# Two hybrid diffusion layers on one core: probabilities scaled by ScalarE and VectorE, output groups in turn, and a reordered start

## The chip, the core and the metric

The kernel runs on one core of a Trainium2 chip. Its time is the device time of one execution in microseconds; each figure for "time" is a median over runs. The trace comes from one separate, profiled execution.

## The reference: what is computed

Two layers over 384 tokens (128 context, 256 latent) of width 1024, in fp32. A layer is: a SwiGLU FFN (hidden width 2816) at half weight, a token mixer, and a second FFN; each takes an RMS-normalised input that is scaled and shifted by adaLN vectors, and each output is gated by one of them.

```python
mod = jax.nn.silu(cvec) @ lp["ada_w"] + lp["ada_b"]
sh1, sc1, g1, sh2, sc2, g2, sh3, sc3, g3 = jnp.split(mod[:, None, :], N_ADA, axis=-1)
h = _rmsnorm(x, lp["norm_g"][0]) * (1.0 + sc1) + sh1
x = x + 0.5 * g1 * _swiglu(h, w1[0], w3[0], w2[0])
h = _rmsnorm(x, lp["norm_g"][1]) * (1.0 + sc2) + sh2
y, ctx = mixer(h)
x = x + g2 * y
```

The mixer projects `h` once and feeds three groups: Hyena (256 channels: a short convolution, then a long one by FFT with a generated filter, two gates), neighbourhood attention N (6 heads of 64, a learned bias over the latent grid), and windowed attention G (6 query heads, 2 key heads, rotary, a sink). Latent tokens also read all cached context keys in the same softmax. The three outputs, 1024 wide together, go through one output projection.

## The kernel before, in words

Tokens are the free dimension: the state is `xT[0..7]`, eight chunks of 128 channels by 384 tokens. Every fp32 product is three TensorE passes in fp32r (`mm3`, lines 291 to 295): high half by high half, and the two mixed ones. Weights arrive by SP's DMA queue into one of three raw buffers in the order of the list `jobs` (lines 135 to 150); `ahead` (line 162) splits them three blocks ahead into `whi` (ScalarE, line 132) and `wlo` (VectorE, line 133). The split stands in the queues of these two engines at the place where `ahead` is called, so the written order is the order of each engine.

adaLN's vectors are 256 reductions on VectorE (`junk`, line 196). `ada_tick` calls them at the rates `RATE` and `MIXRATE`; `need` calls those that are due and not done. The first FFN's own vectors come from TensorE in three chunks (`adm`) whose weights `chunk_load` fetches.

The order of a layer is `ffn(l, 0)`, `mixer(l)`, `ffn(l, 1)`. An FFN begins with eight dense steps `k` of six outputs each, whose inputs are the halves `mh[k]`, `ml[k]`; statistics are taken after step 2 (`stats1`, a sum by TensorE, then an rsqrt by Newton steps that POOL does) and spread over the partitions after step 4 (`stats2`: `dg`, then `pr`). In the very first FFN, `start` is called ahead of each step: it holds the filter generator of Hyena (`first` to `fourth`, `taps`, eight calls of `spectrum`, line 593) and the normalisation of the input (`start_x`, `start_h`).

The mixer first does Hyena's projection: two groups `grp` of four weight blocks `kb`, into six accumulators. Then generators of small steps run beside the matmuls (`work`, `drain`): the convolution and FFT of Hyena, and the normalisation of queries and keys. The projections are called in the order q, k, (kv, gq); gq are the queries of G, which `rot` turns into `ra`, TensorE transposes into `gt`, and ScalarE copies into `qTG`.

Attention is a pipeline over 12 units: N then G, three head pairs, two blocks of 128 queries. The unit with `qi` = 0 also holds the context's queries, so it has n = 2 score blocks, the one with `qi` = 1 has n = 1. Call number s of `slot` does, in this order: scores and masks of unit s (`un_score`), the division by the sum of unit s-1 (`un_norm`, on POOL, line 899), the product with the values of unit s-3 if that had `qi` = 1 (`un_pv`, which ends with `yh`, `yl`), the transposes of unit s-2 and their copies `PT` (`un_turn`, lines 960 to 965), the exponentials of unit s (`un_exp`).

The output projection has three groups of output chunks: 0 to 2, 3 to 5, and 6, 7. `piece(po, g, k)` adds input chunk k to group g between slots: 2 to 7 come from attention, 0 and 1 from Hyena. The pieces of groups 0 and 1 alternate, k = 0 and 1 come last. `update` (line 370) adds a finished chunk to `xT` and `after` calls `square_chunk` and `prep_chunk`, which make the second FFN's `mh`, `ml`.

## Time and profile before

| | |
|---|---|
| median of 3 runs | 1580.31 us (1577.92 to 1580.56) |
| the profiled execution | 1582.27 us, of which the span is 1580.5 |
| mean granted TensorE clock | 0.985 |
| TensorE busy | 1518.8 us (96%), 8616 matmuls |
| VectorE, ScalarE, POOL busy | 1109.9, 675.9, 148.8 us |
| HBM traffic | 257.34 MB read, 164 GB/s over the span |

A row of a timeline begins with start and length in us, then engine, line of the program, operation, tiles and shape; a bracket at its end is the idle time before it and what ended that. "PEld" is the loading of weights into TensorE, "SPq" SP's queue of DMA issues. A pass of the large products is short against its listed length, since passes overlap: what counts is the distance between starts.

### The profile page before, as it was taken

The numbers are of one execution on the slowest core, as the hardware profiler recorded it, in microseconds if no ns is written. First come the engines' busy times: TensorE is split into PE (matmuls) and PEld (weight loads), VectorE is DVE, ScalarE is ACT, GpSimd is POOL, SyncE is SP. The second block draws the span as 40 slices with busy tenths as digits, with TensorE's granted clock in tenths as the row PEclk, the third lists the DMA queues.
The fourth block names the chain that finished last, engine by engine and source line by source line (L and its number), as shares of the span: only waits on it lengthen the run. The fifth ranks groups of instructions, "written<-read, shape, count | busy, mean of one in ns | idle before, by whom it ended". The sixth has DMA issues, their size and how long they took to land.

```text
span 1580.5 us, 23068 instructions
## 1 busy us (share of the span) xinstructions
PE 1518.8 (96%) x8616; PEld 1446.2 (92%) x8616; DVE 1109.9 (70%) x2048; ACT 675.9 (43%) x1237; POOL 148.8 (9%) x266
## 2 busy tenths in 40 slices
PE   6999999999989899999999999999998889999999
PEld 2899999999767799999999999999996689999998
DVE  4469998878765588877858898887776367644433
ACT  4633333336554554333335333343564555433321
POOL 0000000011543000000000000000145500000000
PEclk9999999999999899999999999999998999999999
DMA  9555666565412245655544565556452033433442
GB/s 305 187 189 214 233 229 217 215 212 155 139 36 75 97 138 195 231 210 186 200 145 140 204 245 199 214 203 217 144 162 66 25 113 127 148 137 129 126 140 68
DMA packets 89720, 261.46 MB, mean 165 GB/s; under 512 B 10182, under 2 KB 27656, under 8 KB 89480
## 3 DMA queue, kind: packets, MB, share of 16 engines
q1 hardware_dynamic: 89224, 258.95, 47.8%
q8 instruction: 67, 1.10, 0.3%
q0 software_dynamic: 384, 1.05, 0.2%
q14 instruction: 45, 0.37, 0.1%
HBM read 257.34 MB, written 2.62 MB: 164 GB/s over the span
## 4 chain that ended last, share of the span: by engine, by line
PE 82%; DVE 7%; ACT 6%; POOL 2%; issue 2%; DMA 1%; SPq 0%; DVEq 0%; ACTq 0%; POOLq 0%
PE up L293 14%; PE up L294 14%; PE up L295 14%; PE dn L294 8%; PE dn L293 8%; PE dn L295 8%; PE pj L293 2%; PE pj L295 2%; PE pj L294 2%; DVE wlo L133 2%; POOL pr L899 1%; ACT whi L132 1%; PE sc L911 1%; PE kf L593 1%; PE hy L293 1%
## 5 line engine op out<-in xcount | busy, mean ns | idle before, releaser
L133 DVE TENSOR_TENSOR wlo<-raw,whi 128x1024 fp32r<-128x1024 f32 (+2 forms) x352 | 395.3, 1126 | 170.2 <-ACT whi L132 169.7
L293 PE MATMUL up<-mh,whi 128*128 128x384 f32 (+1 forms) x1408 | 481.0, 342 | 13.4 <-DVE xT L373 6.4
L132 ACT ACTIVATE whi<-raw 128x1024 fp32r<-128x1024 f32 (+2 forms) x352 | 340.9, 976 | 323.6 <-DMA raw<-w 120.8
L295 PE MATMUL up<-mh,wlo 128*128 128x384 f32 (+1 forms) x1408 | 478.2, 340 | 1.0 <-DVE wlo L133 0.8
L294 PE MATMUL up<-ml,whi 128*128 128x384 f32 (+1 forms) x1408 | 477.6, 339 | 0.6 <-DVE ml L133 0.6
L196 DVE CUSTOM_DVE_ANT_0 junk<-adaw,cb,sml 128x1024 bf16<-128x1024 f32 x256 | 332.5, 1299 | 2.2
L293 PEld LDWEIGHTS up<-mh,whi 128*128 128x128 f32 x1408 | 266.2, 189 | 20.2 <-issue 9.3
L295 PEld LDWEIGHTS up<-mh,wlo 128*128 128x128 f32 x1408 | 266.2, 189 | 3.9 <-DVE wlo L133 3.9
L294 PEld LDWEIGHTS up<-ml,whi 128*128 128x128 f32 x1408 | 266.1, 189 | 2.2 <-DVE ml L133 1.3
L294 PE MATMUL dn<-gl,whi 128*128 128x384 f32 x704 | 237.2, 337 | 0.0
L293 PE MATMUL dn<-gh,whi 128*128 128x384 f32 x704 | 237.1, 337 | 0.0
L295 PE MATMUL dn<-gh,wlo 128*128 128x384 f32 x704 | 237.1, 337 | 0.0
L132 ACT ACTIVATE gh<-t 128x384 fp32r<-128x384 f32 x76 | 39.9, 525 | 247.2 <-DVE t L473 239.0
L293 PEld LDWEIGHTS dn<-gh,whi 128*128 128x128 f32 x704 | 132.2, 188 | 0.0
L295 PEld LDWEIGHTS dn<-gh,wlo 128*128 128x128 f32 x704 | 132.2, 188 | 0.0
L294 PEld LDWEIGHTS dn<-gl,whi 128*128 128x128 f32 x704 | 132.1, 188 | 0.0
L303 POOL TENSOR_SCALAR rs_r<-rs_r 128x3 int32<-128x3 int32 (+2 forms) x14 | 6.4, 460 | 1080.3 <-DVE rs_r L302 989.2
L899 POOL TENSOR_SCALAR pr<-pr,nm 128x384 f32<-128x384 f32 x72 | 78.8, 1112 | 65.5 <-DVE nm L896 29.5
L293 PE MATMUL pj<-whi,mh 128*128 128x384 f32 (+1 forms) x240 | 81.1, 338 | 2.0 <-DVE hyt L350 1.1
L295 PE MATMUL pj<-whi,ml 128*128 128x384 f32 (+1 forms) x240 | 78.9, 329 | 0.0
L294 PE MATMUL pj<-wlo,mh 128*128 128x384 f32 (+1 forms) x240 | 78.7, 328 | 0.0
L473 DVE TENSOR_TENSOR t<-up,t 128x384 f32<-128x384 f32 x72 | 39.9, 554 | 49.8 <-PE up L295 49.7
(220 smaller groups left out, 1618.0 us busy)
## 6 DMA issues: line engine op xcount, KB each, us to landing
raw<-w SPq DMA_DIRECT2D x184, 512.0 KB, 4.4
adaw<-ada SPq DMA_DIRECT2D x128, 512.0 KB, 3.5
raw<-w SPq DMA_DIRECT2D x64, 448.0 KB, 4.3
raw<-win SPq DMA_DIRECT2D x48, 384.0 KB, 3.6
raw<-w13a SPq DMA_DIRECT2D x32, 384.0 KB, 4.0
adw<-ada SPq DMA_DIRECT2D x32, 192.0 KB, 4.6
raw<-woa SPq DMA_DIRECT2D x16, 384.0 KB, 3.3
nab<-nab SPq DMA_DIRECT2D x24, 192.0 KB, 3.5
```

The lines of the kernel that those rows point to most:

```text
L132: S.activation(hi, src, AF.Copy)
L133: V.tensor_tensor(lo, src, hi.bitcast(F32), op=ALU.subtract)
L196: V.tensor_tensor_reduce(out=junk, in0=w, in1=cb[:, v, :], scale=scale, scalar=small("ada_b", (l * NADA + p) * KD + j), op0=ALU.mult, op1= ...
L293: T.matmul(out, ah, bh, start=start, stop=False)
L294: T.matmul(out, ah, bl, start=False, stop=False)
L295: T.matmul(out, al, bh, start=False, stop=stop)
L303: G.tensor_scalar(r.bitcast(I32), r.bitcast(I32), -1.0, float(0x5F3759DF), op0=ALU.mult, op1=ALU.add)
L473: V.tensor_tensor(t1, PQ[1][:, :NT], t1, op=ALU.mult)
L593: T.matmul(o, mat[:, 0:1] if row else mat, self.sd[t][:, which].rearrange("p l c -> p (l c)"), start=(n == 0), stop=(n == len(mats) - 1),)
L899: nc.gpsimd.tensor_scalar(pr[:, :w], pr[:, :w], rec[:, e * n + c:e * n + c + 1], None, op0=ALU.mult)
L911: T.matmul(u.sc[e][:, :NT], q[o[e], qs], k1[o[e]], start=True, stop=True)
```

## The change

1. **Rates** of the adaLN reductions: a little more in the first FFN of layer 0, less in the mixer.
2. **Hyena's projection**: statistics after the second block, their rsqrt on VectorE, `stats2` after the third, then `explicit`, `settle` and `deferred` spread over the rest.
3. **Weight order** follows the order of the projections and of the output pieces.
4. **Start**: all squares ahead of the third sine layer, statistics and the first table chunk earlier, `taps(2)` later, the eight spectra each in the middle of one of the eight dense steps.
5. **Convolution**: the first tap on ScalarE.
6. **Scaling of the probabilities**: on ScalarE for units with n = 1 (two operations each), on VectorE for units with n = 2 (four each).
7. **Projections** in the order q, k, gq, kv.
8. **Output groups**: only group 0 has pieces between the slots (k = 2 to 7); Hyena's k = 0, 1 follow, updates 0 to 2; then the whole of group 1 and updates 3 to 5; then group 2 and updates 6, 7.

```diff
--- before.py
+++ after.py
@@ -28,13 +28,12 @@
...
 NADAB = 3
-RATE = ((0.8, 0.72), (0.63, 0.515), (0.69, 0.66), (0.065, 0))
-MIXRATE = ((0.75, 0, 0.5), (0.3, 0, 0.3))
+RATE = ((0.82, 0.74), (0.63, 0.515), (0.69, 0.66), (0.065, 0))
+MIXRATE = ((0.25, 0, 0.5), (0, 0, 0.3))
 BUD = (2.0, 3.0, 1.9)
...
 DLATE = 8
-HYS = (1, 0)
 STAT = ((0, 2), (2, 4))
...
@@ -140,12 +139,12 @@
...
             if f == 0:
-                for g in (0, 1, 2, 3, 6, 5, 4):
+                for g in (0, 1, 2, 3, 5, 6, 4):
                     if g == 6:
...
                         jobs += [(A["win"][l, g, :, k * 768:(k + 1) * 768], 768) for k in range(4)]
-                for g, k in ((0, 1), (0, 2), (0, 3), (1, 1), (1, 2), (1, 3), (0, 0), (1, 0)):
+                for g, k in ((0, 1), (0, 2), (0, 3), (0, 0), (1, 0), (1, 1), (1, 2), (1, 3)):
                     jobs.append((A["woa"][l, g, :, k * 768:(k + 1) * 768], 768))
...
@@ -523,6 +522,8 @@
...
             self.decay = [decay[:, t * HY:(t + 1) * HY] for t in range(3)]
+
+        def load_d(self):
             self.dft0 = load(A["dft0"][:, 0:2 * P], tt("dft0", w=2 * P))
...
@@ -570,7 +571,7 @@
...
             if t < 2:
-                p0 = [ps("tap0") for _ in range(DEPTH)]
+                p0 = [ps("tap0", "a") for _ in range(DEPTH)]
                 for l in range(DEPTH):
...
@@ -660,7 +661,9 @@
...
             w3 = [small("conv_w", (l * 3 + q) * 6 + n) for q in range(3)]
-            V.tensor_scalar(o[:, 1:386], up[:, 0:385], w3[0], small("conv_b", l * 6 + n), op0=ALU.mult, op1=ALU.add)
+            S.activation(
+                o[:, 1:386], up[:, 0:385], AF.Identity, scale=w3[0], bias=small("conv_b", l * 6 + n)
+            )
             for q in (1, 2):
...
@@ -677,20 +680,18 @@
...
                 ahead()
-                if (grp, kb) == (0, HYS[0]):
-                    rs = stats1()
-                if (grp, kb) == (0, 3):
-                    dg = spread_r(rs)
-                ada_tick(MIXRATE[l][grp])
-                if (grp, kb) == (1, HYS[1]):
-                    R = stats2(rs, dg)
-                if grp == 1 and kb > HYS[1]:
-                    n = KD // (3 - HYS[1]) if HYS[1] != 0 else 3
-                    c = kb - HYS[1] - 1
-                    hn = explicit(l, 1, R, range(n * c, min(n * c + n, KD)))
-                    settle(hk)
-                    hk = hn
-                    tm[c] = deferred(pu[c], R, "hyt")
+                s = grp * 4 + kb
+                if s == 1:
+                    dg = spread_r(stats1(V))
+                elif s == 2:
+                    R = stats2(None, dg)
+                if s < 3:
+                    ada_tick(MIXRATE[l][0])
+                elif s < 6:
+                    hk += explicit(l, 1, R, range(3 * (s - 3), min(3 * (s - 2), KD)))
+                if s > 4:
+                    settle(hk[3 * (s - 5):3 * (s - 4)])
+                    tm[s - 5] = deferred(pu[s - 5], R, "hyt")
...
@@ -699,8 +700,6 @@
...
         def conv_bg():
-            settle(hk)
-            yield 1.0
             for n in [n for n in range(6) if n not in tm]:
...
@@ -896,7 +895,11 @@
...
                 for c, (pr, w) in enumerate(u.pr[e]):
-                    nc.gpsimd.tensor_scalar(pr[:, :w], pr[:, :w], rec[:, e * n + c:e * n + c + 1], None, op0=ALU.mult)
+                    r = rec[:, e * n + c:e * n + c + 1]
+                    if n == 1:
+                        S.activation(pr[:, :w], pr[:, :w], AF.Copy, scale=r)
+                    else:
+                        V.tensor_scalar(pr[:, :w], pr[:, :w], r, None, op0=ALU.mult)
...
@@ -1084,24 +1087,33 @@
...
+        pg = project(384, 2, BUD[0])
+        gq_it = add(gq_post(pg), True)
         pkv = project(256, 4, BUD[1])
         gk_it = add(gk_post(pkv), True)
-        pg = project(384, 2, BUD[0])
-        gq_it = add(gq_post(pg), True)
-
-        held = {}
-
-        def piece(po, g, k):
-            kb, kk = divmod(k, 2)
-            if (g, kb) not in held:
-                held[g, kb] = get()
-            hi, lo = held[g, kb]
+
+        def wout_block(po, n, kper, ks, first, last, run=True):
+            hi, lo = get()
+            for kk, i in order2(kper, n, last):
+                s = slice((kk * n + i) * P, (kk * n + i + 1) * P)
+                mm3(
+                    po[i][:, :NT], (hi[:, s], lo[:, s]), Y[ks + kk], first and kk == 0, last and kk == kper - 1
+                )
+            if run:
+                ahead()
+
+        held = []
+
+        def piece(po, k):
+            if not held:
+                held.append(get())
+            hi, lo = held[0]
             for i in range(3):
-                s = slice(kk * 384 + i * P, kk * 384 + (i + 1) * P)
-                mm3(po[i][:, :NT], (hi[:, s], lo[:, s]), Y[k], k == 2, k == 1)
-            if kk:
-                del held[g, kb]
-            ahead(state["cur"] + min(AHEAD, NSPL - len(held)))
+                s = slice(((k % 2) * 3 + i) * P, ((k % 2) * 3 + i + 1) * P)
+                mm3(po[i][:, :NT], (hi[:, s], lo[:, s]), Y[k], k == 2, False)
+            if k % 2:
+                held.pop()
+            ahead()
...
@@ -1111,49 +1123,35 @@
...
         nc.gpsimd.dma_start(out=A["o_nv"][l], in_=X["vN"][0])
-        po = [[ps(f"po{i}", "a") for i in range(3)]]
+        po = [ps(f"po{i}", "a") for i in range(3)]
         slot()
-        piece(po[0], 0, 2)
+        piece(po, 2)
         slot()
+        drain(gq_it)
         drain(gk_it)
-        drain(gq_it)
-        for k in (3, 4, 5):
+        for k in (3, 4, 5, 6):
             slot()
-            piece(po[0], 0, k)
+            piece(po, k)
             slot()
         slot()
-        piece(po[0], 0, 6)
-        slot()
-        spare[0] = "a"
-        po.append([ps(f"po{i}", "b") for i in range(3)])
-        piece(po[1], 1, 2)
-        slot()
-        for g, k in ((1, 3), (0, 7), (1, 4), (1, 5), (1, 6), (1, 7)):
-            piece(po[g], g, k)
-            work(BUD[2])
-            ada_tick(MIXRATE[l][2])
+        piece(po, 7)
         drain(hy_it)
-        for g in range(2):
-            for k in range(2):
-                piece(po[g], g, k)
-            for i in range(3):
-                update(l, 5, 3 * g + i, po[g][i])
-                after(3 * g + i)
-        po = [ps(f"po{i}", "ab"[i]) for i in range(2)]
-        for kb in range(2):
-            hi, lo = get()
-            for kk, i in order2(4, 2, kb == 1):
-                k = kb * 4 + kk
-                s = slice((kk * 2 + i) * P, (kk * 2 + i + 1) * P)
-                mm3(po[i][:, :NT], (hi[:, s], lo[:, s]), Y[k], k == 0, k == KD - 1)
-            if kb == 0:
-                ahead()
-                ada_tick(MIXRATE[l][2])
-        for i in range(2):
-            update(l, 5, 6 + i, po[i])
-            after(6 + i)
+        wout_block(po, 3, 2, 0, False, True, False)
+        for i in range(3):
+            update(l, 5, i, po[i])
+            after(i)
             if i == 0:
                 ahead()
+        for g, n, kper in ((1, 3, 2), (2, 2, 4)):
+            po = [ps(f"po{i}", "b" if g == 1 else "ab"[i]) for i in range(n)]
+            for kb in range(KD // kper):
+                wout_block(po, n, kper, kb * kper, kb == 0, kb == KD // kper - 1, kb < KD // kper - 1)
+                ada_tick(MIXRATE[l][2])
+            for i in range(n):
+                update(l, 5, 3 * g + i, po[i])
+                after(3 * g + i)
+                if i == 0:
+                    ahead()
...
@@ -1174,6 +1172,7 @@
...
                 chunk_rows((j + 2) // 3)
+            F.spectrum(*divmod(j, 3))
             return
...
@@ -1184,35 +1183,30 @@
...
             chunk_load(0)
+            F.load_d()
             issue(2)
...
             F.second()
-            square_chunk(4)
+            for c in range(4, KD):
+                square_chunk(c)
             F.third()
-            for c in range(5, KD):
-                square_chunk(c)
+            r = stats1()
             F.fourth()
...
             F.taps(0)
-            r = stats1()
             F.taps(1)
-            F.taps(2)
-            chunk_load(1)
             ada_tables(0)
-            F.spectrum(0, 0)
-            F.spectrum(0, 1)
-            F.spectrum(0, 2)
+            chunk_rows(0)
             R = stats2(r)
-            ahead(1)
-            chunk_rows(0)
             for c in range(3):
                 start_x(c, R)
-            F.spectrum(1, 0)
+            chunk_load(1)
             chunk_cols(0)
-            F.spectrum(1, 1)
+            ahead(1)
             start_h(0)
+            F.taps(2)
             start_h(1)
...
@@ -1224,8 +1218,6 @@
...
             start_h(j + 1)
-        if j < 4:
-            F.spectrum(*((1, 2), (2, 0), (2, 1))[j - 1])
         if j == 6:
...
         elif j == 7:
```

Three places of the engines' orders. First, ScalarE in the attention of layer 0, among the G units; `yh<-py` is the input of an output piece, `PT` the copy of the transposes, `pr` a unit's probabilities. Before:

```order
L945 ACTIVATE pr_4605,nm<-pr_4605,nm 128x384
L945 ACTIVATE pr_4606,nm<-pr_4606,nm 128x384
L949 ACTIVATE nm<-nm 128x2
L132 ACTIVATE yh_4659<-py 128x384
L965 ACTIVATE PT<-pp_4664 128x512
L965 ACTIVATE PT<-pp_4670 128x512
L939 ACTIVATE pr_4637,nm<-sc_4630,nm 128x128
L939 ACTIVATE pr_4637,nm<-sc_4631,nm 128x128
```

and now:

```order
L900 ACTIVATE pr_4600<-pr_4600,nm 128x384
L900 ACTIVATE pr_4601<-pr_4601,nm 128x384
L131 ACTIVATE yh_4654<-py 128x384
L968 ACTIVATE PT<-pp_4659 128x512
L968 ACTIVATE PT<-pp_4665 128x512
L942 ACTIVATE pr_4632,nm<-sc_4625,nm 128x128
```

Two scalings (line 900 of the changed kernel) now stand directly ahead of `yh` and of both copies `PT`.

Second, VectorE between the third and the fourth update of layer 0's mixer (`xT_86`, `xT_87` are chunks 2 and 3 of the state). Before:

```order
L133 TENSOR_TENSOR ml_113<-m,mh_105 128x384
L133 TENSOR_TENSOR ml_113<-mod_97,mh_105 128x2
L133 TENSOR_TENSOR wlo<-raw,whi 128x768
L373 SCALAR_TENSOR_TENSOR xT_87<-po_4871,mod_97,xT_87 128x128
L373 SCALAR_TENSOR_TENSOR xT_87<-po_4871,mod_97,xT_87 128x256
```

and now:

```order
L132 TENSOR_TENSOR ml_113<-m,mh_105 128x384
L132 TENSOR_TENSOR ml_113<-mod_97,mh_105 128x2
L132 TENSOR_TENSOR wlo<-raw,whi 128x768
L195 ISA junk,gsc_99<-adaw,cb,sml 128x1024
L195 ISA gsc_99 128x1
L132 TENSOR_TENSOR wlo<-raw,whi 128x1024
L195 ISA junk,gsc_99<-adaw,cb,sml 128x1024
L195 ISA gsc_99 128x1
L214 TENSOR_TENSOR gsc_99<-gsc_99,sml 128x2
L132 TENSOR_TENSOR wlo<-raw,whi 128x1024
```

The updates of group 1, which followed those of group 0 with one weight split between, now have splits and adaLN reductions ahead of them.

Third, ScalarE in the first dense steps; `mh_106` is the input of the fourth step, `xr` its chunk before the split. Before:

```order
L132 ACTIVATE whi<-raw 128x768
L1161 ACTIVATE xr<-xr,mod_97,gsc_99 128x128
L1161 ACTIVATE xr<-xr,mod_97,gsc_99 128x256
L132 ACTIVATE mh_106<-xr 128x384
L599 ACTIVATE kft_95<-kf,sml 128x256
```

and now:

```order
L600 ACTIVATE kft_95<-kf,sml 128x256
L600 ACTIVATE kft_96<-kf,sml 128x256
L131 ACTIVATE whi<-raw 128x768
L1159 ACTIVATE xr<-xr,mod_97,gsc_99 128x128
L1159 ACTIVATE xr<-xr,mod_97,gsc_99 128x256
L131 ACTIVATE mh_106<-xr 128x384
```

The weight split still stands ahead of the chunk of the fourth step, and copies of a spectrum (`kft`) now come ahead of it in each step.

## Rows read from the trace of the kernel before

**Rows 1.** The page: span, busy time of each engine, chain that ended last by engine.
```profile
span 1580.5 us, 23068 instructions
...
PE 1518.8 (96%) x8616; PEld 1446.2 (92%) x8616; DVE 1109.9 (70%) x2048; ACT 675.9 (43%) x1237; POOL 148.8 (9%) x266
...
PE 82%; DVE 7%; ACT 6%; POOL 2%; issue 2%; DMA 1%; SPq 0%; DVEq 0%; ACTq 0%; POOLq 0%
```
**Rows 2.** Windows: stretch, length, busy (instructions) by engine, clock, DMA share, GB/s.
```profile
core 0: us, PE busy (x) PEld busy (x) DVE busy (x) ACT busy (x) POOL busy (x), PEclk, DMA share, GB/s
120.00:160.00 40.00, 40.00 (x230) 40.00 (x229) 36.79 (x55) 13.90 (x20) 0.00 (x0) 1.00 0.61 224
0.00:40.00 40.00, 25.52 (x99) 11.02 (x99) 18.64 (x54) 18.56 (x41) 2.73 (x17) 1.00 0.91 303
404.30:458.00 53.70, 44.66 (x239) 35.59 (x237) 36.07 (x105) 28.38 (x75) 25.91 (x39) 0.91 0.35 110
458.00:499.40 41.40, 36.76 (x230) 25.41 (x229) 16.96 (x66) 22.68 (x67) 20.68 (x20) 0.95 0.07 23
523.60:553.20 29.60, 22.73 (x101) 19.72 (x100) 17.46 (x39) 13.69 (x31) 3.17 (x13) 0.83 0.27 87
```
**Rows 3.** Waits of PE: us in total, times, longest us.
```profile
PE pp L960 <- POOL pr L899: 13.0, 16, 2.1
PE gt L774 <- DVE ra L1032: 9.3, 2, 4.6
PE up L293 <- DVE xT L373: 6.4, 5, 1.9
PE up L293 <- ACT mh L132: 3.7, 3, 2.4
PE pr L341 <- DVE dg L335: 1.9, 2, 1.3
PE pp L962 <- POOL pr L899: 1.4, 2, 0.9
PE pj L293 <- DVE hyt L350: 1.1, 2, 0.6
PE pj L293 <- ACT mh L132: 0.9, 1, 0.9
```
**Rows 4.** Timeline 39 to 59 us (start, length), and the page's DMA issues.
```profile
39.99 0.44 PE L293 MATMUL up<-mh,whi 128*128 128x384 f32 x1 [2.35 <-ACT mh L132]
...
57.24 1.88 PE L593 MATMUL kf<-taps,dftl 128*128 128x512 f32 x4
58.55 0.74 PE L293 MATMUL up<-mh,whi 128*128 128x384 f32 x1
...
43.32 9.51 SPq L100 DMA_DIRECT2D raw<-w13a  x4
...
raw<-w13a SPq DMA_DIRECT2D x32, 384.0 KB, 4.0
```
**Rows 5.** Lines by form: busy us, mean ns, idle before and its releasers.
```profile
L899 POOL TENSOR_SCALAR pr<-pr,nm 128x384 f32<-128x384 f32 x48 | 61.4, 1284 | 65.5 <-DVE nm L896 29.5 <-PE sc L914 12.0 <-ACT pr L945 7.5
L945 ACT ACTIVATE pr<-pr,nm 128x384 f32<-128x384 f32 x48 | 29.1, 613 | 11.2 <-DVE nm L922 8.0 <-DVE nm L932 2.9
L663 DVE TENSOR_SCALAR uc<-up,sml 128x385 f32<-128x385 f32 x12 | 5.8, 481 | 1.7 <-ACT up L658 0.6
```
**Rows 6.** Timelines of the passages: VectorE and TensorE at 499 and 527 to 544, TensorE at 1262 and 1304 us.
```profile
527.35 0.74 DVE L373 SCALAR_TENSOR_TENSOR xT<-po,mod,xT 128x128 f32<-128x128 f32 x2
530.47 0.73 DVE L373 SCALAR_TENSOR_TENSOR xT<-po,mod,xT 128x128 f32<-128x128 f32 x2
533.86 0.96 DVE L133 TENSOR_TENSOR wlo<-raw,whi 128x768 fp32r<-128x768 f32 x1 [0.20 <-ACT whi L132]
534.74 1.28 DVE L196 CUSTOM_DVE_ANT_0 junk<-adaw,cb,sml 128x1024 bf16<-128x1024 f32 x1
...
499.42 0.44 PE L293 MATMUL po<-yh,whi 128*128 128x384 f32 x1
543.44 0.72 PE L329 MATMUL pss<-ones,accq 128*128 128x1 f32 x6
544.02 0.42 PE L293 MATMUL up<-mh,whi 128*128 128x386 f32 x1
...
1262.60 0.44 PE L293 MATMUL po<-yh,whi 128*128 128x384 f32 x1
1304.76 0.42 PE L293 MATMUL up<-mh,whi 128*128 128x386 f32 x1
```

## The prediction, written before the changed kernel ran

> **What bounds the kernel now.** First the page: of a span of 1580.5 us TensorE is busy for 1518.8, and 82% of the chain that ended last is PE's own, with VectorE (7%) and ScalarE (6%) next [rows 1]. So the time is PE's work plus the pieces in which it stands still. The windows tell where those are: 120 to 160 us, dense FFN steps, hold 40.00 us of PE in 40.00, 230 first passes, 0.174 us for each; nothing can be won there. The first 40 us hold 25.52, the two halves of layer 0's attention 44.66 of 53.70 and 36.76 of 41.40, the passage from its mixer to the FFN 22.73 of 29.60 [rows 2]. The list of PE's waits tells who ends its idle time: POOL's scaling `pr` (13.0 and 1.4 us), the rotated queries `ra` (9.3), the updates of `xT` (6.4), `mh` (3.7), and in hyena's projection `dg` (1.9), `hyt` (1.1) and `mh` (0.9) [rows 3]. The change touches each of these, so the question is what is late next. The sum is made against the profiled execution, 1582.27 us (its span and 1.8 around it), 2.0 above the median of 1580.31; the forecast is median plus sum.
>
> **Start: -0.6.** The first dense product begins at 39.99 us, after five of the eight spectra; one spectrum inside a step holds PE from 57.24 to 58.55, 1.3 us [rows 4]. With those five moved behind it, and the statistics and table chunk ahead of them, I estimate a first product near 30 us (39.99 less the five's 6 to 7 us and 3 us of waits between them). That looks like 10 us, but weights bound it: the fifth raw piece is issued at 43.32, behind the table transfers of SP's queue, none of which goes, and its kind lands in 4.0 us [rows 4], so at 47.3. Its ScalarE half stands in the new order ahead of `xr` and `mh` of the fourth step, whose product waits for both: 0.8 for the half, 1.0 and 0.5 for `xr` and `mh`, some 1.4 for VectorE's work between, 51. Now that step begins at 58.55 with all spectra behind it; then, five are left, 5×1.35 = 6.75. Gain 58.55-51-6.75 = 0.8, taken as 0.6. Bounds: -5.7 if the piece doesn't gate and the step begins at 46; +2 if VectorE is late as well.
>
> **Hyena's projection: -2.** VectorE takes over the rsqrt: 15 operations of 0.16 to 0.19 us and `dg`, 3×0.28, 3.5 us. PE's `pr`, two blocks of work behind the sums before and one now, waits some 0.8 us for that per layer, 1.6. What goes are `dg`, `hyt` and `mh`, 1.9+1.1+0.9 = 3.9 [rows 3]. -2.3, taken as **-2**; bounds -3.9 and, if the pieces of `explicit` squeezed between weight splits make three small waits a layer, +2. The convolution's first tap (12 × 0.48 us [rows 5]) goes from VectorE to a ScalarE that is busy for 28.38 of 53.70 us there [rows 2], and the other adaLN rates move the same reductions between dense steps: nothing, since the next due work is PE's.
>
> **Attention: 0.** POOL's scaling takes 1284 ns for 384 columns [rows 5]. On ScalarE the nearest row of that shape is the exponential, 613 ns; on VectorE the multiplication of 385 columns, 481 ns [rows 5]. Both are faster than POOL, and PE's waits on POOL go: -14.4. With the queries of the second kind projected third, `gt` no longer waits for `ra`, 4.6 at a time [rows 3], but for ScalarE, whose copies of queries stand ahead of those of `kTG` in the new order; I leave 2.6 of it per layer: -4. What is late next: POOL was a queue of its own, and nothing stood behind the scaling there. Now the two scalings of a one-block unit (six per layer) stand on ScalarE ahead of `yh`, for which the output piece waits, and of `PT`; and they wait for a reciprocal that VectorE does behind the next unit's masks of 0.55 us. Price of a slot: nothing, if the reciprocal is early and PE has enough of its own work; 2.5, if both scalings (1.2) and two masks with the reciprocal (1.3) show; I take the scalings alone, 1.2, since masks and PE's scores begin together. 12×1.2 = +14.4. The last piece, k = 7, now follows its own `yh` with nothing between: about 2 a layer, +4. Sum -14.4-4+14.4+4 = **0**, bounds -18 and +16. The Trainium skill ("PSUM — Partial Sum Buffer", section "Engine vs sequencer instructions") calls the queues of ScalarE, VectorE and GpSimdE strictly first in, first out; by that sentence alone the price is at its upper end whenever the reciprocal is late, and it is the mechanism of case C. No row of before shows a scaling on ScalarE.
>
> **Mixer to FFN: -7.4.** A chunk's update, square, sum and halves are a chain between VectorE and ScalarE; from one update to the next it takes 527.35 to 530.47, 3.12 us [rows 6], so eight take 25. In it VectorE also splits weights (0.96 us, 533.86) and reduces adaLN vectors (1.28, 534.74) [rows 6]. From the attention's last piece, 499.42, to the FFN's fourth step, 544.02 (after the statistics at 543.44), it is 44.6 us [rows 6], for 192 passes of 0.176 and 0.65 of statistics, 34.4: 10.2 are lost. Layer 1, 1262.60 to 1304.76 [rows 6], 42.2: 7.8 lost. Before, the first three updates come when only 18 passes and the last group's 48 are left beside six updates; now the first three come when 120 passes are left, the next three run beside 48. From `k = 7` on it is 201 passes, 36.0 us with the statistics. VectorE's row order for the stretch, 25 us of chunks, wait for the first outputs, splits and 6 reductions (layer 1: 3) instead of 7 (5), I add up to 43.3 and 39.3. Lost 7.3 and 3.3: gains 2.9+4.5 = **7.4**. Bounds: 0, if the chain's start is as late as before; -15, if PE never waits (all but 3).
>
> **Sum.** -0.6-2+0-7.4 = **-10**: 1580.3-10 = 1570.
>
> **Rivals.** *A, the forecast:* **1570**, chance 0.43.
>
> *B, the waits go and nothing follows:* 14.4+9.3+6.4+3.9 [rows 3] and 5.0 of the start, -39, **1541**. For it: ScalarE is busy 43% of the span [rows 1], and while PE stands still its clock falls, 0.83 granted in 523.6 to 553.2, 0.91 in 404.3 to 458 [rows 2], so that less idling pays twice. Against it: what the order shows behind the scaling, and that chain of 25 us. Chance 0.22.
>
> *C, slower: the scaling in ScalarE's order holds up the output pieces.* Place: `yh` of the even slots, six a layer. Price: 2.5 each, 30 us, and 4 for k = 7, less 14.4 and 4 of waits that go and 10 of the other parts: +6, **1586**. It decides when the scaling ends later than PE's scores, `py` and transposes of the slot in most of them; that is when VectorE, with 24 scalings of its own more, has a backlog. Against: VectorE is busy 36.07 of 53.70 and 16.96 of 41.40 us there [rows 2]. Chance 0.20.
>
> *D, no change:* hyena's pieces k = 0, 1 still stand ahead of every update, eight chunks of 3.12 us follow whatever the order, and the other edits cancel: **1580**, chance 0.15.
>
> **Range and chances.** 0.2%, 3.2 us, is about what a measurement of this kernel can tell from no change. The range of 8 in 10 goes from 1550 (A with the best ends of start and passage, -5 and -8 more, and the mildest of B) to 1587 (C): it leaves out most of B below and the worst of C. Faster by over 0.2%: A but for 0.03, B, and 0.02 of D, 0.64; slower: nearly all of C, and 0.02 of D, 0.21; within: 0.15.
>
> **What would show it.** Right: PE's waits on POOL's scaling gone, waits on `yh`, `PT` and ScalarE's scaling of 14 to 22 us in their place; the first dense product near 30 us but the fourth step near 51; `gt` waiting 2 to 3 us a layer; from k = 7 to the fourth FFN step 43 and 39 us. Wrong: the fourth dense step at 46 (the weight doesn't gate); pieces that follow their slot without waiting (B); over 2 us ahead of most pieces (C); updates that begin as late as before (D).

## The result, and the profile after

The changed kernel takes 1593.38 us (median of 4 runs, 1592.38 to 1593.99) where the kernel before takes 1579.12 in the same series (4 runs): the ratio is 1.009, with a 95% interval of 1.0072 to 1.0107. It is 14.3 us slower; 10 us faster was forecast, and the time lies above the forecast's range of 1550 to 1587. One of e2's four runs below took 1689.23 us at a granted clock of 0.843 and is left out of its median; with it the median is 1589.95, from which two of the expectations take 3.4 us for the start. The profiled execution took 1593.26 us, 11.0 more than that of before.

The page and TensorE's list of waits (us in total, times, longest us) of the changed kernel:

```profile
span 1591.3 us, 22952 instructions
...
PE 1515.8 (95%) x8616; PEld 1446.4 (91%) x8616; DVE 1118.7 (70%) x2110; ACT 690.9 (43%) x1273; POOL 55.1 (3%) x168
```
```profile
PE po L292 <- ACT yh L131: 17.6, 10, 2.9
PE up L292 <- ACT mh L131: 7.8, 4, 5.1
PE pj L292 <- ACT pj L735: 5.6, 2, 2.8
PE up L292 <- ACT whi L131: 5.3, 4, 1.8
PE pp L963 <- DVE yd L832: 4.8, 2, 2.4
...
PE sc L914 <- ACT kTG L1087: 4.1, 2, 2.0
PE cv L845 <- ACT PT L968: 3.3, 4, 1.4
...
PE up L292 <- DVE xT L372: 1.3, 1, 1.3
```

TensorE has the same 8616 matmuls. The waits that the change was aimed at are gone or small: no wait on POOL, none of `gt` on `ra`, 1.3 us on `xT` instead of 6.4 [rows 3]. In their place stand waits on ScalarE: 17.6 us of output pieces on `yh`, 5.6 us of the projection on `pj`, and 4.8 us of transposes (`pp`) on VectorE's operation `yd`, a product of Hyena's FFT that stands behind the scaling in VectorE's order.

Where the time came from is read by the starts of the stages, the first `up`, `dn`, `hy`, `pj` in the timelines of both kernels (us; "change" is the length after less the length before):

| stage | start before | start after | length before | length after | change |
|---|---|---|---|---|---|
| to the first `dn` of layer 0 | 0 | 0 | 237.06 | 241.17 | +4.1 |
| `hy` to `pj`, layer 0 | 329.37 | 333.62 | 27.91 | 27.58 | -0.3 |
| `pj` to the second FFN's `up` | 357.28 | 361.20 | 166.34 | 171.81 | +5.5 |
| that `up` to its `dn` | 523.62 | 533.01 | 200.52 | 197.51 | -3.0 |
| `hy` to `pj`, layer 1 | 1095.94 | 1101.62 | 26.81 | 27.57 | +0.8 |
| `pj` to `up`, layer 1 | 1122.75 | 1129.19 | 164.06 | 171.82 | +7.8 |
| `up` to `dn`, layer 1 | 1286.81 | 1301.01 | 197.60 | 193.79 | -3.8 |

The stages left out differ by 0.4 us at most. So the start and both mixers are longer, and only the entry of the second FFN is shorter.

**The start.** Timeline of TensorE, ScalarE and SP's queue about the fourth dense step (start, length), and windows of the same stretch (columns as in rows 2):

```profile
48.45 0.84 ACT L131 ACTIVATE whi<-raw 128x768 fp32r<-128x768 f32 x1 [5.83 <-DMA raw<-w13a]
50.67 0.98 ACT L1159 ACTIVATE xr<-xr,mod,gsc 128x128 f32<-128x128 f32 x2 [1.38 <-DVE mod L287]
51.68 0.52 ACT L131 ACTIVATE mh<-xr 128x384 fp32r<-128x384 f32 x1
...
52.26 0.69 PE L292 MATMUL up<-mh,whi 128*128 128x384 f32 x1 [5.10 <-ACT mh L131]
52.85 0.69 PE L293 MATMUL up<-ml,whi 128*128 128x384 f32 x1
...
55.58 2.09 PE L594 MATMUL kf<-taps,dftl 128*128 128x512 f32 x4
57.10 0.74 PE L292 MATMUL up<-mh,whi 128*128 128x384 f32 x1
...
43.49 1.34 SPq L99 DMA_DIRECT2D raw<-w13a  x3
```
```profile
52.26:60.00 7.74, 7.74 (x28) 6.41 (x29) 2.74 (x4) 5.08 (x11) 0.00 (x0) 0.76 0.29 94
```

The fifth weight piece is issued at 43.49 us, as before [rows 4]; its split on ScalarE waits 5.83 us for it and holds back `xr` and `mh`, and the fourth step begins at 52.26. The nine passes behind that idle stretch take 3.32 us, to 55.58, where nine passes at full clock take about 1.6: the granted clock of 52.26 to 60 us is 0.76. With the spectra that are left, it is 188.91 us from the fourth step to the first `dn`, where before it was 178.51 (58.55 [rows 4] to 237.06): 10.4 more, for which the forecast had 6.75.

**The mixer.** First the projections: ScalarE, TensorE and, last, VectorE in layer 0, timeline.

```profile
380.31 0.71 ACT L664 ACTIVATE uc<-up,sml 128x385 f32<-128x385 f32 x1 [1.44 <-DVE up L657]
...
383.36 0.71 ACT L664 ACTIVATE uc<-up,sml 128x385 f32<-128x385 f32 x1 [0.91 <-DVE up L657]
...
388.31 0.71 ACT L664 ACTIVATE uc<-up,sml 128x385 f32<-128x385 f32 x1 [2.81 <-DVE up L657]
388.92 0.83 ACT L131 ACTIVATE whi<-raw 128x768 fp32r<-128x768 f32 x1
389.66 1.23 ACT L735 ACTIVATE pj<-pj 128x384 f32<-128x384 f32 x3
...
390.18 0.44 PE L292 MATMUL pj<-whi,mh 128*128 128x384 f32 x1 [2.81 <-ACT pj L735]
...
386.69 1.50 DVE L765 TENSOR_TENSOR pj<-pj,rs_r 128x384 f32<-128x384 f32 x3 [0.42 <-POOL rs_r L307]
388.13 0.08 DVE L657 MEMSET up<- 128x1 f32 x3
```

The convolution's first tap (line 664), now ScalarE's, waits three times in these rows for the memsets of its input's zero columns (line 657), which are VectorE's. The third and longest time, 2.81 us, those stand on VectorE behind a multiplication that itself waits for POOL's rsqrt; the first two times they stand behind VectorE's other work, reductions and the splitting of a weight. The copies of the key projection out of its accumulators (line 735) stand on ScalarE behind the tap, and the next projection on TensorE waits for these accumulators. On the kernel before, ScalarE's part of the convolution waited for nobody there.

Then the slots. ScalarE, VectorE and TensorE about the first output piece of layer 0, timeline:

```profile
450.47 1.12 ACT L900 ACTIVATE pr<-pr,nm 128x384 f32<-128x384 f32 x2 [3.39 <-DVE nm L895]
451.50 0.47 ACT L131 ACTIVATE yh<-py 128x384 fp32r<-128x384 f32 x1
...
450.22 0.16 DVE L895 RECIPROCAL nm<-nm 128x2 f32<-128x2 f32 x1
452.00 0.56 DVE L132 TENSOR_TENSOR yl<-py,yh 128x384 fp32r<-128x384 f32 x1 [1.62 <-ACT yh L131]
...
452.02 0.69 PE L292 MATMUL po<-yh,whi 128*128 128x384 f32 x1 [2.88 <-ACT yh L131]
```

ScalarE is idle for 3.39 us until VectorE's reciprocal, then scales for 1.12 us, and only then makes `yh`; the piece `po` waits 2.88 us for it. This is the place that case C named. The reciprocal at 450.22 comes right behind the masks of the next unit, as the forecast had it.

**From mixer to FFN.** Last attention piece and fourth FFN step of both layers, TensorE's timeline:

```profile
506.50 0.44 PE L292 MATMUL po<-yh,whi 128*128 128x384 f32 x1 [0.58 <-ACT yh L131]
...
551.28 0.42 PE L292 MATMUL up<-mh,whi 128*128 128x386 f32 x1
...
1274.48 0.44 PE L292 MATMUL po<-yh,whi 128*128 128x384 f32 x1 [0.58 <-ACT yh L131]
...
1316.67 0.42 PE L292 MATMUL up<-mh,whi 128*128 128x386 f32 x1
```

44.78 and 42.19 us, for 201 passes where 44.60 and 42.16 held 192 [rows 6]: with the nine passes (1.6 us) taken off, 1.4 and 1.6 us less.

### The profile page after: what moved, and what is told of

It is laid out like the page before. It is cut to its first block, busy times and chain, and to the rows that moved or that the text cites. A ratio compares the mean times of both kernels' runs of the same rounds, so it can differ in the third digit from the quotient of the medians.

```text
span 1591.3 us, 22952 instructions
## 1 busy us (share of the span) xinstructions
PE 1515.8 (95%) x8616; PEld 1446.4 (91%) x8616; DVE 1118.7 (70%) x2110; ACT 690.9 (43%) x1273; POOL 55.1 (3%) x168
## 4 chain that ended last, share of the span: by engine, by line
PE 78%; DVE 10%; ACT 6%; issue 2%; DMA 1%; POOL 1%; SPq 0%; DVEq 0%; ACTq 0%
PE up L292 14%; PE up L294 14%; PE up L293 14%; PE dn L293 8%; PE dn L294 8%; PE dn L292 8%; DVE wlo L132 2%; PE pj L292 2%; PE pj L294 2%; PE pj L293 2%; ACT whi L131 1%; DVE pr L925 1%; PE hy L292 1%; PE hy L293 1%; PE hy L294 1%
## 5 line engine op out<-in xcount | busy, mean ns | idle before, releaser
L292 PE MATMUL up<-mh,whi 128*128 128x384 f32 (+1 forms) x1408 | 482.0, 342 | 14.4 <-ACT mh L131 7.8
L132 DVE TENSOR_TENSOR gl<-t,gh 128x384 fp32r<-128x384 f32 x76 | 42.4, 558 | 45.0 <-ACT gh L131 45.0
L313 ACT ACTIVATE sq<-xT 128x384 f32<-128x384 f32 x42 | 22.0, 525 | 105.2 <-DVE xT L372 104.9
```

Of the source, the lines that this page charges most:

```text
L132: V.tensor_tensor(lo, src, hi.bitcast(F32), op=ALU.subtract)
L292: T.matmul(out, ah, bh, start=start, stop=False)
L313: S.activation(sq, xT[j], AF.Square)
```

## The experiments

Two theories stood at the outset. Theory 1: four things, each with its own cause, make up the result: the start's weight piece (about 4 us), the tap's wait for VectorE (about 9), the scaling's exchange of POOL's waits for ScalarE's, and a smaller gain at the FFN's entry. Theory 2: the scaling on ScalarE is all of it. The first four runs undo one part each on the changed kernel. All differences are between medians; "after" is 1593.4 us.

**e1: the tap back on VectorE.**

```diff
-            S.activation(
-                o[:, 1:386], up[:, 0:385], AF.Identity, scale=w3[0], bias=small("conv_b", l * 6 + n)
-            )
+            V.tensor_scalar(o[:, 1:386], up[:, 0:385], w3[0], small("conv_b", l * 6 + n), op0=ALU.mult, op1=ALU.add)
```

> The changed kernel with the convolution's first tap back on VectorE, all else as changed. Theory 1 (the tap on ScalarE waits for VectorE's three memsets, which stand behind normalisations that wait for POOL's rsqrt; ScalarE's copies of the projection's banks stand behind the tap, and TensorE for those banks: 2.8 us of idling per layer and about 1.8 us of passes at the lower clock behind it): 9 us faster than the changed kernel, near 1584 us, and TensorE's wait for the copy `pj` (5.6 us in two) gone. Theory 2 (all that is lost comes from the scaling on ScalarE, 17.6 us of waits on `yh`): within 2 us of the changed kernel.

Measured: 1584.52 us, 8.9 faster than after. The wait on `pj` is gone from the list, and from `pj` to the first score it takes 50.82 us where after took 55.41 (layer 1: 50.76 and 55.43). The tap on ScalarE costs 8.9 us.

**e2: the start as before.** `start`, the loads of `load_d` and the tag of `tap0` are those of the kernel before.

> The changed kernel with the start as before (order of squares, taps, chunks and spectra), all else as changed. Theory 1 (the fourth dense step waits for the fifth weight piece whatever the start does, five spectra now come behind it, and the idle time costs clock): 4 us faster than the changed kernel, near 1589 us, the first `dn` back near 237 us after the span's start. Theory 2 (the start is neutral, the loss lies in the mixers): within 1.5 us of the changed kernel.

Measured: 1588.99 us, 4.4 faster; the first `dn` begins at 237.90 us instead of 241.17. Theory 1.

**e3: all scalings on VectorE.**

```diff
-                    if n == 1:
-                        S.activation(pr[:, :w], pr[:, :w], AF.Copy, scale=r)
-                    else:
-                        V.tensor_scalar(pr[:, :w], pr[:, :w], r, None, op0=ALU.mult)
+                    V.tensor_scalar(pr[:, :w], pr[:, :w], r, None, op0=ALU.mult)
```

> The changed kernel with all scalings on VectorE, none on ScalarE. In the changed kernel four scalings took VectorE 1.14 us together and two took ScalarE 1.12. Theory 1 (the output pieces wait for `yh`, which stands on ScalarE behind two scalings that wait for a reciprocal): most of the 17.6 us of waits on `yh` go, some 10 us faster than the changed kernel, near 1583. Theory 2 (VectorE is the bound in the attention: its masks are late, whoever scales): within 3 us, with the waits shifted to transposes that wait for VectorE.

Measured: 1573.76 us, 19.6 faster than after, twice what was expected, and faster than the kernel before (ratio 0.9963, 0.9953 to 0.9974). The waits on `yh` are gone; in their place the pieces wait for VectorE's half, 10.5 us:

```profile
PE po L293 <- DVE yl L132: 10.5, 10, 2.4
```

**e4: all scalings on POOL again.** The same place, with `nc.gpsimd.tensor_scalar`.

> The changed kernel with all scalings on POOL again. Theory 1 (moving the scaling exchanged waits on POOL, 14.4 us, for waits on ScalarE of about the same size): within 4 us of the changed kernel, with waits of the transposes on POOL of 10 to 15 us in place of those on `yh`. Theory 2 (the scaling on ScalarE is what made the kernel slower): 14 us faster or more, near 1579.

Measured: 1583.32 us, 10.1 faster. Neither theory hits the number: theory 1 said within 4, theory 2 14 or more. The waits exchange as theory 1 says, but not at par:

```profile
PE pp L960 <- POOL pr L899: 10.9, 16, 1.0
...
PE po L292 <- ACT yh L131: 1.2, 2, 0.6
```

POOL's 11.7 us (10.9 and 0.8 in a second row) and 2.4 on `yh` and on `cv` for `PT` (1.2 each) stand against 17.6 on `yh`, 4.8 on `yd` and 3.3 on `cv` in the changed kernel, 11.6 less, which is about the time gained. The clock does not explain it: its mean is 0.986 here and 0.987 in the changed kernel. So the division of the scaling between ScalarE and VectorE costs 10.1 us against POOL, where the forecast's own terms for it (-14.4, +14.4 and +4) made 4.

**e5: memsets on POOL.** Is it the wait for VectorE or the tap's length on ScalarE?

```diff
-                V.memset(up[:, c:c + 1], 0.0)
+                nc.gpsimd.memset(up[:, c:c + 1], 0.0)
```

> The changed kernel, the tap still on ScalarE, but the three memsets of its input on POOL instead of VectorE. Theory 1 (ScalarE waits for VectorE's queue at the memsets, and that wait is what holds up the copies of the projection's banks): most of what putting the tap back on VectorE gave (8.9 us) comes, 5 to 9 us faster than the changed kernel, and ScalarE's wait ahead of the last tap before the copies shrinks from 2.8 us. Theory 2 (it is the tap's own length on ScalarE, 0.71 us each): within 2 us of the changed kernel, TensorE's wait on `pj` stays at 2.8 us a layer.

Measured: 1591.43 us, 2.0 faster, the wait on `pj` 5.4 us. By its wording theory 2; but the trace shows that the test was no test. ScalarE's timeline:

```profile
383.98 0.71 ACT L664 ACTIVATE uc<-up,sml 128x385 f32<-128x385 f32 x1 [5.47 <-POOL up L657]
```

The memsets stand on POOL behind the very rsqrt that VectorE's multiplication had waited for, so the tap waited for POOL instead.

**e9: zeros from ScalarE itself.** The same question, with a tap that waits for no other queue.

```diff
-                V.memset(up[:, c:c + 1], 0.0)
+                S.activation(up[:, c:c + 1], tm[n][0][:, 0:1], AF.Copy, scale=0.0)
```

> The changed kernel, the tap on ScalarE, but the three zero columns of its input written by ScalarE itself (three more short operations of about 0.2 us per convolution), so that the tap waits for no other engine. The run with the memsets on POOL put them behind POOL's rsqrt and so only exchanged the wait. Theory 1 (ScalarE's wait for another engine's queue is the cost): 5 to 9 us faster than the changed kernel, near 1586, and TensorE's wait on the copy `pj` gone. Theory 2 (the tap's own 0.71 us on ScalarE is the cost): slower by 0 to 3 us, the wait on `pj` 2.8 us or more a layer.

Measured: 1583.51 us, 9.9 faster, though ScalarE does 4.5 us more. The wait on `pj` is gone. The same tap, before and now (lines by form, after and e9):

```profile
L664 ACT ACTIVATE uc<-up,sml 128x385 f32<-128x385 f32 x12 | 8.5, 710 | 11.8 <-DVE up L657 11.7
```
```profile
L664 ACT ACTIVATE uc<-up,sml 128x385 f32<-128x385 f32 x12 | 8.5, 712 | 0.4
```

The tap takes ScalarE just as long; its 11.7 us of waiting are what went. That VectorE is rid of the memsets is not what helps: e5 took the same memsets off it and gained 2.0. The cost of part 5 is the wait, not the work.

**e6: the third table chunk later.**

```diff
             issue(4)
-            chunk_load(2)
...
+        if j == 2:
+            chunk_load(2)
         if j in (2, 5):
```

> The changed kernel with the third table chunk (16 transfers) loaded two dense steps later, so that the fifth weight piece stands ahead of it on SP's queue. Theory 1 (the fourth dense step waits for that piece): it is issued before 36 us instead of 43.5, the fourth step begins at 47 to 48 instead of 52.3 and without the lower clock behind it; 5 to 7 us faster than the changed kernel, near 1587. Theory 2 (VectorE's and ScalarE's work for the input is late as well): under 2 us.

Measured: 1586.57 us, 6.8 faster. Timeline of SP's queue and TensorE:

```profile
31.57 9.62 SPq L99 DMA_DIRECT2D raw<-w13a  x5
...
47.80 0.34 PE L292 MATMUL up<-mh,whi 128*128 128x384 f32 x1
```

SP's queue issues five weight pieces between 31.57 and 41.19 us, ahead of the chunk; the step that began at 52.26 begins at 47.80 without a wait, and the first `dn` at 234.78. So the new start is good for 2.3 us against the kernel before (237.06) once the weight is there, and the weight was what made it 4.1 worse.

**e10: output groups as before.** Groups 0 and 1 in alternating pieces, k = 0 and 1 last, weights in that order.

> The changed kernel with the output groups and their weights' order as before (groups 0 and 1 in alternating pieces, k = 0 and 1 last). Theory 1 (the new order of the groups is worth what the traces show from the last attention piece to the fourth FFN step, 1.4 and 1.6 us): 2 to 4 us slower than the changed kernel, near 1596. Theory 2 (the pieces that the old order has between and behind the slots give ScalarE time for `yh`; the change took that cover away): faster than the changed kernel by 3 us or more, with less waiting on `yh`.

Measured: 1595.5 us, 2.1 slower. Theory 1: the new order of groups is worth 2.1 us here, and 6.4 us of `up` waiting for `xT` return.

**e11: kv ahead of gq, as before.**

> The changed kernel with kv projected before gq, as before. Theory 1 (the first G scores wait for ScalarE's `kTG`, 2.05 us a layer, instead of `gt` for `ra`, 4.6): about 5 us slower, near 1598, with waits of `gt` on `ra` of 4 to 5 us a layer. Theory 2 (only the name of the wait changed): within 2 us.

Measured: 1601.34 us, 8.0 slower. TensorE's waits:

```profile
PE gt L773 <- DVE ra L1035: 10.4, 2, 5.2
...
PE gk L773 <- ACT PT L968: 8.1, 2, 4.0
```

Part 7 is worth 8.0 us in the changed kernel, twice the forecast's 4. The second row, the transposes of the keys (`gk`), is not in the list of the kernel before, though that has the same order of projections; it comes with the divided scaling, as e13 shows. So part of the 8.0 seems to be a cost of part 6 that part 7 avoids; no run takes the two apart.

**e7: the kernel before, with the scaling on VectorE.** One line, as in e3, in the old order.

> The kernel before with nothing changed but the scaling, on VectorE instead of POOL. From the runs so far, scaling on VectorE is 9.6 us faster than on POOL in the changed order. Theory 1 (that gain belongs to the scaling, whatever the order of the output groups): 8 to 12 us faster than the kernel before, near 1569. Theory 2 (it needs the new order, since in the old one VectorE's masks and `ra` are late): under 3 us.

Measured: 1561.57 us, 17.0 faster than before (ratio 0.9895, 0.9876 to 0.9914). Theory 1 and more.

**e8: start as before, tap and scalings on VectorE.**

> The changed kernel with the start as before, the tap back on VectorE, and all scalings on VectorE. If the three losses are independent, 1593.4 - 3.4 - 8.9 - 19.6 = 1561.5; if they share VectorE's time (theory 2: the tap and the scaling both go there), 1566 to 1570.

Measured: 1560.42 us, 33.0 faster than after; the three single runs make 4.4 + 8.9 + 19.6 = 32.9, so they do not share a bound. But this is the one-line e7 to within 1.2 us: with the scaling on VectorE, the reordered output, projections and statistics together bring next to nothing against the old order. What e10 and e11 give for parts 8 and 7 (2.1 and 8.0) holds in the changed kernel, with its divided scaling, and need not hold beyond it.

**e12: tap and scalings on VectorE, weight early, everything else as changed.**

> The changed kernel with all scalings and the tap on VectorE and the third table chunk loaded later: the three losses mended and the new start kept. From the single runs: 1560.4 (scaling and tap on VectorE with the old start) less the 3.4 us by which the new start with early weights beats the old one, 1557. If the new start's gain is hidden elsewhere, 1560 to 1562.

Measured: 1558.15 us, ratio to before 0.9868 (0.9853 to 0.9882). By the single runs the new start with early weights beats the old one by 2.4 us (1588.99 less 1586.57), which makes 1558.0. It is the lowest median of the study, faster than both kernels, by 35.2 us against the changed one.

**e13: the kernel before, with the scaling divided as in the change.**

> The kernel before with nothing changed but the scaling, split between ScalarE (units of one block) and VectorE as in the change. In the changed order that split costs 10.1 us against POOL. Theory 1 (the cost belongs to the scaling's place ahead of `yh` on ScalarE, whatever the groups do): slower than the kernel before by 5 to 12 us, near 1587. Theory 2 (the old order of pieces covers it, and the cost comes from the new groups): from 5 us faster to no change.

Measured: 1588.53 us, 9.3 slower than before. TensorE's waits:

```profile
PE po L293 <- ACT yh L132: 11.7, 8, 2.7
...
PE gk L774 <- ACT PT L969: 4.0, 1, 4.0
PE gk L774 <- DMA nab<-nab: 4.0, 1, 4.0
PE pp L964 <- DVE yc L835: 3.4, 2, 1.7
```

The pieces wait for `yh` there too. So the cost of the divided scaling does not come from the new groups. But the 11.7 us on `yh` are less than POOL's 14.4 that went [rows 3]: the loss shows only with the 8.0 us on `gk` and 3.4 on `yc`, which the kernel before does not have. That `yh` alone is the cost, as theory 1 has it, is not shown in this order.

**e14: the same operations, the scaling behind `yh`.** The scalings of one-block units are issued after `un_pv`; ScalarE does the same work.

```diff
+            if 0 <= s - 1 < len(hs) and hs[s - 1].n == 1:
+                un_scale(hs[s - 1])
```

> The changed kernel, the same operations on the same engines, but in each slot ScalarE's two scalings are issued behind the product with the values and its `yh` instead of ahead of them. Theory 1 (the output piece waits because `yh` stands behind a scaling that waits for VectorE's reciprocal): the 17.6 us of waits on `yh` fall below 5, 10 to 17 us faster than the changed kernel, near 1580. Theory 2 (ScalarE is simply too busy, 1.12 us more per slot): within 4 us, the wait moved to `PT`.

Measured: 1583.77 us, 9.6 faster, just short of the 10 to 17 that theory 1 named and far beyond theory 2's 4. Waits on `yh` fell from 17.6 to 1.2 us; 6.0 on VectorE's half and more on `PT` came:

```profile
PE po L293 <- DVE yl L132: 6.0, 6, 1.6
PE cv L845 <- ACT PT L974: 4.8, 4, 1.3
PE sc L920 <- ACT PT L974: 2.7, 2, 1.4
```

So in the changed kernel nearly all of the scaling's cost against POOL (10.1) is its place in ScalarE's order, not its work.

## Why the prediction was wrong

The sign was wrong. By its own steps, with what each step cost or gave in the changed kernel (positive is slower; from undoing it, or from the stages):

| step | forecast | measured | from |
|---|---|---|---|
| start | -0.6 | +4.4 | e2 |
| hyena's projection | -2 | +0.4 | stages `hy` to `pj` |
| convolution's tap | 0 | +8.9 | e1 |
| scaling off POOL | +4 (-14.4+14.4+4) | +10.1 | e4 |
| queries third | -4 | -8.0 | e11 |
| output groups | -7.4 | -2.1 | e10 |
| sum | -10 | +13.7 | against +14.3 |

The 0.6 us that the sum leaves lie within the spread of the runs. The rates and the weight order were not tried alone, and the parts lean on each other (e8, e11), so it is partly luck that the sum comes out so well.

- **The step that failed most** is the sentence that the tap goes "to a ScalarE that is busy for 28.38 of 53.70 us there ... nothing". An idle share was taken for cover. It was also the share of another stretch: the first tap starts at 375.49 us, ahead of that window. What decided was that the tap waits for VectorE's memsets and that the projection's copies stand behind it; VectorE's and ScalarE's orders show both, and no bound was given. It cost 8.9 us, and e9 shows that the wait is all of it.
- **The scaling.** The forecast named the mechanism and placed it on the right instruction. Five slots of layer 0 wait 2.88, 0, 1.89, 2.73 and 0.73 us, the last piece 0.58, so 8.8 a layer and 17.6 in all, against 14.4 and 4. That total is nearly met, by luck in part: a slot costs more than the 1.2 us taken and the last piece less than 2. The term that failed is what the three make together, +4, for which 10.1 was measured (e4). Left out were 4.8 us of transposes that wait for VectorE's `yd` and 3.3 us of `cv` that wait for `PT`, and POOL's waits were worth 11.7 in the new order, not 14.4. With all scalings on VectorE (e3) or on POOL (e4) no transpose waits for `yd`. It is not that `yd` is earlier: in e3 it starts at 435.06 us, where in the changed kernel it starts at 434.18, and the same transposes start at 434.02 without it. Why they have to wait for it only with the divided scaling is open.
- **The start.** The mechanism is right: the fifth piece at 43.49, the fourth step at 52.26 against a forecast 51. The step "five are left, 5×1.35" fell short: 10.4 us instead of 6.75, part of it nine passes at 3.32 us behind 5.1 us of idling. The rows of before could have warned of that price: three stretches in which TensorE idles have a granted clock of 0.91, 0.95 and 0.83, though the first 40 us have 1.00 [rows 2].
- **Output groups.** Forecast from the last piece to the fourth step: 43.3 and 39.3 us; measured 44.78 and 42.19. The chain of updates is as long as it was said to be, but its second half can't begin before group 1 is done: ScalarE stands idle 7.35 us for chunk 3's update,

```profile
529.89 0.52 ACT L313 ACTIVATE sq<-xT 128x384 f32<-128x384 f32 x1 [7.35 <-DVE xT L372]
```

  and five chunks, weight halves and two reductions then follow in series.
- **Queries third** were better than forecast: 2.05 us of waiting a layer are left, as said (2.6), but with the old order in the changed kernel the waits on `ra` would have been 5.2 us a layer and the transposes of the keys late too, so that the part is worth 8.0 there (and, by e8, not in every kernel).
- **The rivals.** C, at 0.20, comes nearest, by sign, place and sort of wait; its price was put at 30 us for twelve slots, and it was held unlikely because VectorE had spare time. But its own sign, over 2 us ahead of most pieces, did not come: two pieces in six of a layer wait that long. And no rival holds the tap's 8.9 us, without which (e1) the kernel is at 1584.5, close to C's 1586. The signs named for the forecast mostly came true (no wait on POOL, 17.6 us on `yh`, a first dense product at 29.89 us, the fourth step at 52.26), and none of them looked at the place where most was lost. VectorE's reciprocal was late all the same: ScalarE waited for it in all twelve slots,

```profile
ACT pr L900 <- DVE nm L895: 33.5, 12, 5.1
```

  2.8 us each. Spare time on the average says nothing of when an operation that waits its turn in order is done. The Trainium skill's sentence ("PSUM — Partial Sum Buffer", section "Engine vs sequencer instructions") that these queues are strictly first in, first out was weighed under "Attention" and given too little weight; e14 moves the scaling behind `yh` and wins 9.6 us with nothing else changed, which agrees with it.

## What to carry to other kernels

When an operation moves to an engine that works in order, cost it by its wait: find what it waits for, on which queue that stands, and name every instruction behind it for which the bottleneck engine waits. An engine that is half idle is no cover, and an engine of its own, even three times slower, can be worth more than a place ahead of a critical copy. Before reordering a stage, try the plain alternative for its slowest engine: here one changed line gave 17 us (e7), and the reordering around it about 1 more (e8 against e7).

## What the runs showed of the hardware that was not expected

Scaling by a value per partition, 128x384 in fp32, in SBUF: POOL 1284 ns [rows 5], ScalarE 607, VectorE 417 (128x128: 767 on POOL, 281 on VectorE). Lines by form, after and e7:

```profile
L900 ACT ACTIVATE pr<-pr,nm 128x384 f32<-128x384 f32 x24 | 13.4, 607 | 33.5 <-DVE nm L895 33.5
L902 DVE TENSOR_SCALAR pr<-pr,nm 128x384 f32<-128x384 f32 x24 | 10.0, 417 | 0.4
```
```profile
L899 DVE TENSOR_SCALAR pr<-pr,nm 128x384 f32<-128x384 f32 x48 | 19.0, 417 | 0.8
```

Four of them in one slot, from the timeline of the changed kernel:

```profile
431.07 1.14 DVE L902 TENSOR_SCALAR pr<-pr,nm 128x384 f32<-128x384 f32 x4
```

These four, two wide and two narrow, took 1.14 us together, less than the sum of their own times (1.40), so their listed times overlap. The Trainium skill ("GPSIMD Engine Reference", section "4.1 Engine selection") puts elementwise work with one input on GpSimd at roughly line rate; these rows do not agree, POOL takes three times as long as VectorE. POOL's row is from a kernel in which VectorE works beside it; POOL alone was not run.
